# Output projection as seven products of half blocks, and norm 2 of two row tiles at a time

## The chip, the cores and the metric

The kernel runs on one core of one Trainium2 chip. The metric is device microseconds of one execution. Before the change the median of three runs is 676.44 us (676.13 to 676.68). Engines are called PE (matrix multiplies), DVE (vector), ACT (scalar), POOL (GpSimd) and SP (sync). SP and POOL issue nearly all transfers here; the transfers that add to what lies at their destination are issued by POOL.

## The reference

One decoder layer in fp32, 512 tokens, width 1024, followed by a final norm. Cut to what matters here:

```python
D_MODEL, SEQ, D_FF = 1024, 512, 2816
merged = (sigmoid(ga) * (out_a @ w_branch_swa)        # branch A
          + sigmoid(gd) * (out_d @ w_branch_diff))    # branch D
x = x + gate1 * (merged @ w_out)                      # the output projection
h2 = rmsnorm(x, norm2_g) * (1.0 + scale2) + shift2    # norm 2
u = h2 @ w_up                                         # up projection, 1024 x 5632
a, g = split(u, 2)
a = causal_depthwise_conv(a, conv_w, conv_b)
x = x + gate2 * ((gelu(a) * g) @ w_down)              # down projection
return rmsnorm(x, final_g)
```

`gate1`, `scale2`, `shift2` and `gate2` come from the conditioning vector, one value for each of the 1024 channels.

## The kernel before, in words

**Splitting.** Every fp32 operand is split in two parts (`split`, L119-120): ACT casts it into a rounded part (hi), DVE takes hi from the operand (lo). A product is then three matmuls: hi by hi, hi by lo, lo by hi. So weights go through four steps: load, ACT cast, DVE lo, PE.

**Ahead of the projection.** For each k of eight (128 channels of `merged`), a unit of gate products (`pgd`, `add_gate_d`, L953) and a unit of branch products (`pB`, `add_merge`, L963) run on PE. The merge of k (L982-984) is done on DVE and ACT: (tanh + 1) times the product, plus branch A's part `ta`, split into `mg..h` and `mg..l`.

**The output projection.** The eight rows of `w_out` (`wo`, 128x1024 each) are loaded by SP (L1025), multiplied by gate1 laid out along the rows (`g1b`, DVE, L1026) and split. `out_step(t, k)` (L1251-1260) multiplies row tile t (128 tokens) by row k of the weights into the two banks of t, called `oc`; there are eight banks, all of PSUM. Five of the eight k run over all four tiles, then the last three (`TAIL`) run tile after tile, so that tiles end one after the other: 8 x 4 x 2 x 3 = 192 matmuls of 128x512.

**Norm 2.** As a tile ends, DVE adds its banks to the residual `x1` (`add_x`, L1266); ACT squares both halves and sums the squares (`square2`, L1272); ACT takes the root (`norm_a`, L172), and a chain of small DVE operations gives the reciprocal root (`norm_b`, L174-178, L164-168). `norm_c` scales the tile into `xn` (L1286). PE turns two tiles at a time (`turn2`, L1296, banks `th`), ACT and DVE modulate and split them (`early`, L1304-1321). The last two tiles are scaled by halves on DVE and ACT (`norm_halves`).

**The up projection** already is in seven products of halves (Strassen's scheme in Winograd's form): for each of 11 column pairs J, the slots p1, m5, m6, p2, m7, p3, p4 (`mul_slot`, L1200), each 24 matmuls of 128x256. Their weights are blocks of `w_up` and sums of blocks: `s1` and `s3` are loaded by SP and added to by an accumulating transfer of POOL (`load_raw`, L1100-1102), and the sums for m6 and p3 are made in place by DVE (`sum_w`, L1124). `cast_w` (L1130, ACT) and `low_w` (L1134, DVE) split them. **The down projection** is in seven products too, with weights `chain_..` that grow by accumulating transfers (L1801).

**What sets the order.** Up to the five first k of the projection a scheduler orders the instructions. From L1333 on (`manual_schedule`) PE, DVE, ACT and POOL run in the order in which the code is written, to the end of the column pair J = 1. An engine takes its instructions in that order; one that waits holds up all behind it. SP's loads start when the buffer they write is free.

Of the kernel before, what the change touches and what calls it, by code (L numbers as in the profile page):

```python
# [8 lines left out]
F32 = mybir.dt.float32  # L9
# [5 lines left out]
P = 128  # L15
# [11 lines left out]
WB = 3  # L27
# [20 lines left out]
def kernel(  # L48
# [86 lines left out]
    hold = cpool.tile([P, 1], F32, name="hold")  # L135
# [802 lines left out]
    mg = [[bp.tile([P, 2, S], F32R, tag="gx", bufs=5, name=f"mg{i}{b}") for b in "hl"] for i in range(2)]  # L938
    mg += [[bp.tile([P, 2, S], F32R, tag="gx", bufs=5, name="mg2h"), bp.tile([P, 2, S], F32R, tag="y", name="mg2l")]]
    mg += [[bp.tile([P, 2, S], F32R, tag="fgb", name="mg3h"), gpart(5, [P, 2, S], "mg3l", F32R)]]  # L940
    mgh, mgl = ([mg[k // 2][b][:, k % 2] for k in range(KT)] for b in range(2))
    tdall = gpart(2, [P, 3, S], "tdall")
    tds, merged = {}, []

    g1b = gpart(4, [P, D], "g1b")
# [7 lines left out]
    def add_gate_d(j):  # L953
        def gate(wts):
            o = fbank(f"pgd{j}")
            yield from steps(o, wts, hT, KT)
            tds[j] = tdall[:, j % 3]
            nc.scalar.activation(tds[j], o, AF.Tanh, scale=0.5)

        units.append((lambda: load_tile(TILE_GD + j, f"wgd{j}"), gate))  # L960

    def add_merge(j):
        def load():  # L963
            if j % 2 == 0:
                r = raw_tile([P, 4, 2 * P], f"wbd{j}")
                nc.sync.dma_start(r, wbd[:, j * P : (j + 2) * P].rearrange("(i p) n -> p i n", p=P))
                if j % 4:
                    wb = bp.tile([P, 2, 4, 2 * P], F32R, tag="m5w", name=f"wbd{j}")
                else:
                    wb = gpart(3, [P, 2, 4, 2 * P], f"wbd{j}", F32R)  # L970
                wh, wl = wb[:, 0], wb[:, 1]
                casts[0], lows[0] = split(wh, wl, r)
                recent[:] = recent[1:] + lows
                pair_w["d"] = wh, wl
            return pair_w["d"]

        def branch(wts):
            o = sbank(f"pB{j}")
            rhs = [[vv[b][:, k] for k in range(4)] for b in range(2)]
            yield from steps(o, wts, rhs, 4, cl=slice(j % 2 * P, j % 2 * P + P))  # L980
            td = tds[j]
            merged.append(nc.vector.scalar_tensor_tensor(td, td, 1.0, o, ALU.add, ALU.mult))  # L982
            nc.vector.tensor_add(td, td, ta[:, j])
            split(mgh[j], mgl[j], td)

        units.append((load, branch))

    for j in range(KT):
        add_gate_d(j)
        if j:  # L990
            add_merge(j - 1)
    add_merge(KT - 1)
    while units or loaded or current or later:
        fill(1)
    root_table(tds[KT - 1][:, 0:1])
    for _ in ada:
        fill(1)
    while later:
        fill(1)
    man.close()  # L1000


    def brow(dst, src):
        nc.gpsimd.dma_start(dst, src.partition_broadcast(P))

    TAIL = 3
    xnp = [gpart(i, [P, 2, D], f"xn{i}") for i in range(2)]
    nc.vector.tensor_add(late_mod[:, 8:24], late_mod[:, 8:24], blate[:, 8:24])
    nc.vector.scalar_tensor_tensor(a2c, a2c, 1.0, n2g, ALU.add, ALU.mult)
    nc.vector.tensor_scalar_mul(a2c, a2c, -0.5)  # L1010
    x1 = big.tile([P, NT, D], F32, tag="qa", name="x1")
    for t in range(NT):
        nc.sync.dma_start(x1[:, t], xd[t * P : (t + 1) * P, :])

    def eight(name):
        return [
            [tbank(name + "0"), tbank(name + "1")],
            [fbank(name + "2"), fbank(name + "3")],
            [sbank(name + "4"), sbank(name + "5")],
            [sbank(name + "6"), vbank(name + "7")],  # L1020
        ]

    def load_rows(src, k, name, gate):
        r = raw_tile([P, D], name)
        nc.sync.dma_start(r, src[k * P : (k + 1) * P, :])  # L1025
        nc.vector.tensor_mul(r, r, gate)  # L1026
        return split_pair(r, [P, D], name)

    def tok_proj(acc, lh, ll, wts, nk, done, half_done=None):
        def step(k, t, hfs=(0, 1)):  # L1030
            wh, wl = wts[k]
            a = lh(k)[:, t * P : (t + 1) * P]
            b = ll(k)[:, t * P : (t + 1) * P]
            for hf in hfs:
                sl = slice(hf * S, (hf + 1) * S)
                nc.tensor.matmul(acc[t][hf], a, wh[:, sl], start=k == 0, stop=False)
                nc.tensor.matmul(acc[t][hf], a, wl[:, sl], start=False, stop=False)
            for hf in hfs:
                sl = slice(hf * S, (hf + 1) * S)
                nc.tensor.matmul(acc[t][hf], b, wh[:, sl], start=False, stop=k == nk - 1)  # L1040

        for k in range(nk - TAIL):
            for t in range(NT):
                step(k, t)
# [21 lines left out]
    def add_and_stat(acc, dst, x, wpool, name):  # L1066
# [12 lines left out]
        return rs  # L1079

# [800 lines left out]
```

## Time and profile before

| | |
|---|---|
| median of three runs | 676.44 us |
| the profiled execution | 676.2 us |
| its span in the trace | 674.2 us |
| mean granted PE clock | 0.997 |
| PE busy, of the span | 99% |
| DVE, ACT, POOL busy | 84%, 60%, 13% |
| first product of the output projection starts | 291.85 us |
| its last product starts | 336.17 us |
| bytes moved | 121.78 MB |

Times in the trace count from the start of the span. The profiled execution's own time is 2.0 us longer than its span, and 0.24 us under the median. A group's line names the code line, the engine, the operation, output and inputs, and the shapes. PE's busy time counts a matmul as long as it is in the pipeline, so that consecutive matmuls overlap: the distance from one start to the next is what one costs.

### The profile page before, as it was taken

The page shows a single profiled execution, that of the slowest core. Times are in us where ns is not written, and L with a number is a line of the kernel's source. Part 1 is how long each engine was busy: PE and PEld are TensorE (multiplying, and loading weights), DVE is VectorE, ACT ScalarE, POOL GpSimd, SP SyncE. Part 2 cuts the span into 40 slices and gives each one's busy share as a digit, 9 for nine tenths or more (in the row PEclk, how much of TensorE's full clock was granted, in tenths as well). Part 3 has the DMA queues.
Part 4 walks back from the last instruction along what each step waited for, and adds up shares of the span by engine and source line. Part 5 has one row for each costly group of instructions (what it writes and reads, how often), then busy time and mean ns, then how long its engine had stood idle before and what let it go on. Part 6 is the DMA issues. An engine that isn't in the chain of part 4 may idle for free.

```text
span 674.2 us, 10799 instructions
## 1 busy us (share of the span) xinstructions
PE 664.3 (99%) x4021; PEld 591.7 (88%) x4021; DVE 564.0 (84%) x1006; ACT 401.3 (60%) x705; POOL 85.0 (13%) x111
## 2 busy tenths in 40 slices
PE   8999999999999999999999999999999999999995
PEld 8888888888888888888899999999999998888884
DVE  6988987768777686644899999899889999979996
ACT  7678787465745333233696655556655666665664
POOL 2000000002212100000010211011111004441200
PEclk9999999999999999999999999999999999999998
DMA  9961231445356783367275898997887758997803
GB/s 355 418 238 62 95 95 63 137 145 180 90 168 214 229 306 117 102 181 256 77 120 155 204 203 221 243 227 187 213 212 210 203 188 217 202 206 202 158 0 125
DMA packets 72212, 121.78 MB, mean 181 GB/s; under 512 B 4256, under 2 KB 48448, under 8 KB 72160
## 3 DMA queue, kind: packets, MB, share of 16 engines
q1 hardware_dynamic: 53248, 95.04, 41.3%
q0 software_dynamic: 18624, 25.84, 22.6%
q8 instruction: 31, 0.51, 0.3%
q10 hardware_dynamic: 288, 0.21, 0.1%
q14 instruction: 21, 0.17, 0.1%
HBM read 118.97 MB, written 2.11 MB: 180 GB/s over the span
## 4 chain that ended last, share of the span: by engine, by line
PE 88%; issue 7%; DVE 2%; DMA 2%; POOL 1%; ACT 0%; POOLq 0%
PE up L1200 33%; PE dc L1815 7%; PE av L375 3%; PE pga L123 2%; PE pga L125 2%; PE pga L124 2%; PE pgd L125 2%; PE pgd L123 2%; PE oc L1260 2%; PE oc L1256 2%; PE oc L1257 2%; PE pgd L124 2%; PE aqa L372 2%; PE sd L683 2%; PE sw L585 1%
## 5 line engine op out<-in xcount | busy, mean ns | idle before, releaser
L1200 PE MATMUL up<-t,m_whi 128*128 128x256 f32 x512 | 93.1, 283 | 0.0
L1200 PEld LDWEIGHTS up<-t,m_whi 128*128 128x128 f32 x512 | 79.9, 192 | 0.0
L1200 PE MATMUL up<-t,m_wlo 128*128 128x256 f32 x256 | 72.4, 283 | 0.0
L1200 PE MATMUL up<-bh,p_whi 128*128 128x256 f32 x232 | 65.7, 283 | 0.0
L1200 PE MATMUL up<-bl,p_whi 128*128 128x256 f32 x232 | 65.7, 283 | 0.0
L1200 PE MATMUL up<-bh,p_wlo 128*128 128x256 f32 x232 | 65.7, 283 | 0.0
L1200 PEld LDWEIGHTS up<-t,m_wlo 128*128 128x128 f32 x256 | 49.2, 192 | 0.0
L1102 POOL DMA_DIRECT2D s<-in_w_up_dram x21 | 27.0, 1363 | 158.5 <-DMA s<-in_w_up_dram 95.2
L1200 PEld LDWEIGHTS up<-bh,p_whi 128*128 128x128 f32 x232 | 44.5, 192 | 0.0
L1200 PEld LDWEIGHTS up<-bl,p_whi 128*128 128x128 f32 x232 | 44.5, 192 | 0.0
L1200 PEld LDWEIGHTS up<-bh,p_wlo 128*128 128x128 f32 x232 | 44.5, 192 | 0.0
L1130 ACT CAST m_whi<-s 128x1024 fp32r<-128x1024 f32 x31 | 32.5, 1048 | 18.4 <-DVE s L1124 10.5
L1134 DVE TENSOR_TENSOR m_wlo<-s,m_whi 128x1024 fp32r<-128x1024 f32 x31 | 37.8, 1219 | 1.3 <-ACT m_whi L1130 1.3
L1200 PE MATMUL up<-t,p_whi 128*128 128x256 f32 x176 | 32.2, 283 | 0.0
L799 DVE CUSTOM_DVE_ANT_0 ra<-ra,csb 128x1024 f32<-128x1024 f32 x24 | 29.1, 1220 | 1.3 <-DMA ra<-in_w_ada_t_dram 1.3
L1200 PEld LDWEIGHTS up<-t,p_whi 128*128 128x128 f32 x176 | 27.4, 192 | 0.1
L1130 ACT CAST p_whi<-wa 128x1024 fp32r<-128x1024 f32 x18 | 18.8, 1044 | 14.0 <-PE up L1200 8.6
L709 ACT ACTIVATE sd<-sd,dmx 128x128 f32<-128x128 f32 (+3 forms) x32 | 17.7, 555 | 14.9 <-DVE dmx L694 14.7
L1134 DVE TENSOR_TENSOR p_wlo<-wa,p_whi 128x1024 fp32r<-128x1024 f32 x18 | 22.0, 1222 | 4.0 <-ACT p_whi L1130 3.3
L1200 PE MATMUL up<-t,p_wlo 128*128 128x256 f32 x88 | 24.9, 283 | 0.0
L1124 DVE TENSOR_TENSOR s<-s,wa 128x1024 f32<-128x1024 f32 x20 | 24.4, 1219 | 0.1
L1207 ACT ACTIVATE gT<-a,cols 128x512 f32<-128x512 f32 x22 | 17.5, 812 | 10.1 <-DVE a L1242 9.7
(553 smaller groups left out, 2047.9 us busy)
## 6 DMA issues: line engine op xcount, KB each, us to landing
ra<-in_w_ada_t_dram SPq DMA_DIRECT2D x24, 512.0 KB, 3.9
wa<-in_w_up_dram SPq DMA_DIRECT2D x22, 512.0 KB, 4.5
s<-in_w_up_dram SPq DMA_DIRECT2D x21, 512.0 KB, 5.5
s<-in_w_up_dram POOLq DMA_DIRECT2D x21, 512.0 KB, 7.3
adaw<-in_w_ada_t_dram SPq DMA_DIRECT2D x15, 512.0 KB, 9.8
a<-in_w_up_dram SPq DMA_DIRECT2D x11, 512.0 KB, 4.8
b<-in_w_down_dram SPq DMA_DIRECT2D x10, 512.0 KB, 4.7
w<-in_w_first_dram SPq DMA_DIRECT2D x8, 512.0 KB, 9.9
```

Of the source, the lines that this page charges most:

```text
L123: nc.tensor.matmul(o, lh, rh, start=start, stop=False)
L124: nc.tensor.matmul(o, lh, rl, start=False, stop=False)
L125: nc.tensor.matmul(o, ll, rh, start=False, stop=stop)
L375: nc.tensor.matmul(acc[i], ht[:, t : t + P], wts[k][w][:, S:], start=start, stop=stop)
L709: nc.scalar.activation(pm[m], pm[m], AF.Exp, bias=mx[:, m : m + 1], scale=-1.0, accum_out=(l0, l1)[m])
L799: nc.vector.tensor_tensor_reduce(r, r, csb, 1.0, 0.0, ALU.mult, ALU.add, late_mod[:, idx : idx + 1])
L1102: nc.gpsimd.dma_start(dst, upblock(*blk), accum_op=ALU.add)
L1124: nc.vector.tensor_add(src, src, R[J, "a11" if name == "m6" else "a12"])
L1130: nc.scalar.copy(W[J, name][0], R[J, SRC[name]])
L1134: nc.vector.tensor_sub(lo, R[J, SRC[name]], hi.bitcast(F32))
L1200: nc.tensor.matmul(o[u], w[:, k, cu], b[:, k], start=name in ("p1", "m5", "p2") and k == 0 and x == 0, stop=k == 3 and x == 2, skip_group_ ...
L1815: nc.tensor.matmul((bank2[u] if o is None else o)[:, sl], a[:, q, cu], b[:, q, sl], start=first_mm and x == 0, stop=last_mm and x == 2, sk ...
```

## The change

**Seven products.** `merged` is a 2x2 array of blocks of 512 channels by 256 tokens, `w_out` one of 512x512 blocks. The products m1, m5, m6, p2, p3, m7 and p4 (`prods`, `mul_out`) have 24 matmuls of 128x512 each, 168 in all. Each multiplies a sum of blocks of `merged` by a sum of gated blocks of `w_out`, into one of three pairs of banks: `oU` (m1, m6, m7 and p4, which accumulate on each other), `oV` (m5, p3) and `oX` (p2). Results that more than one block of the output needs are kept: `keep_sum` copies a pair of banks on ACT, and an accumulating transfer adds the copy to `x1`. `merge_x` adds or subtracts a bank in `x1` on DVE, in the place of `add_x`.

**Activations.** The merge of k writes into `M` (the buffers `outh` and `outl`), with one half of the tokens sign-changed; sums of its blocks are made on DVE, and the operands split into `a11`, `a2h`/`a2l`, `opA` and `opB`.

**Weights.** Blocks of 256x512 are loaded by SP, each gated once (`gate_o`, DVE): two of b11 into `chain_o`, two of b12 that go on to a scratch in DRAM, and two each of b22 (`p3raw`) and b21 (`p2raw`). `add_by_dma` makes the sums: POOL issues a transfer that adds one buffer, or the scratch, to another. `piece` splits a sum; the next block is added to the same buffer after that.

**Norm 2** runs on tiles 0 and 1 together, then 2 and 3: statistics two columns wide, the root by `norm_start` on ACT, the rest by `norm_end` (`rstd_end`, L163-168, in its form of several columns).

**Up projection.** For J = 0 the sums for m6 and p3 are made by accumulating transfers, in place of `sum_w`. The slot p1 of J = 1 is whole, its slot p2 stands behind m6 of J = 0. The POOL copy into `hold` is gone. Splits of the first weights (`early_w`) now stand under the branch products.

On PE the end of the projection reads as follows before (the last products of tile 2, the first of tile 3, the transposes `th0` of tiles 0 and 1; `oc4` to `oc7` are the banks of tiles 2 and 3).

```order
L1260 MATMUL oc4_2811<-wo7_h_2867,mg3l_2342 128x512
L1260 MATMUL oc5_2812<-wo7_h_2867,mg3l_2342 128x512
L1256 MATMUL oc6_2813<-wo5_h_2853,mg2h_2339 128x512
L1257 MATMUL oc6_2813<-wo5_l_2854,mg2h_2339 128x512
L1260 MATMUL oc6_2813<-wo5_h_2853,mg2l_2340 128x512
L1296 MATMUL th0_0_3128<-ident_69,xn0_2795 128x128 x4
L1296 MATMUL th0_1_3133<-ident_69,xn0_2795 128x128 x4
L1256 MATMUL oc6_2813<-wo6_h_2860,mg3h_2341 128x512
```

And now (the end of m7, whose weights are `t3p1`; the first half of p4, with weights `t4p0` and `t4p1`; the transposes):

```order
L1178 MATMUL oU1_2879<-t3p1_wlo_3082,op_hhA_2884 128x512
L1178 MATMUL oU1_2879<-t3p1_whi_3081,op_hlA_2885 128x512
L1178 MATMUL oU0_2878<-t4p0_3116,a2h0_2338 128x512 x2
L1178 MATMUL oU0_2878<-t4p0_3116,a2l0_2340 128x512
...
L1178 MATMUL oU0_2878<-t4p1_wlo_3132,a2h1_2339 128x512
L1178 MATMUL oU0_2878<-t4p1_whi_3131,a2l1_2341 128x512
L1293 MATMUL th0_0_3157<-ident_69,xn0_2840 128x128 x4
L1293 MATMUL th0_1_3162<-ident_69,xn0_2840 128x128 x4
L1178 MATMUL oU1_2879<-t4p0_3116,a2h0_2338 128x512 x2
```

The transposes stood among products into another tile's banks; now they stand between the two halves of p4, which adds to the banks that m7 has just written.

On DVE the first adds to `x1` and the norm of tile 0 read as follows before (`sso` are sums of squares, `ms` and `r0` steps of the reciprocal root, `rso` the root).

```order
L1266 TENSOR_TENSOR x1_2800<-x1_2800,oc0_2807 128x512
L1266 TENSOR_TENSOR x1_2800<-x1_2800,oc1_2808 128x512
L1342 TENSOR_TENSOR early2_2873<-wa1_0_2879,early2_2873 128x1024
L1274 TENSOR_SCALAR sso00_3051<-sso00_3051 128x1
L174 SCALAR_TENSOR_TENSOR ms_3059<-sso01_3055,sso00_3051 128x1
L178 RECIPROCAL r0_3057<-r0_3057 128x1
L164 SCALAR_TENSOR_TENSOR rt_3064<-r0_3057,ms_3059 128x1
L168 SCALAR_TENSOR_TENSOR rso0_3062<-rt_3064,r0_3057 128x1
L1286 TENSOR_SCALAR xn0_2795<-x1_2800,rso0_3062 128x1024
L1266 TENSOR_TENSOR x1_2800<-x1_2800,oc2_2809 128x512
```

And now, from the second pair of merges (out of `oV`) on:

```order
L1257 TENSOR_TENSOR x1_2873<-x1_2873,oV0_2880 128x512
L1257 TENSOR_TENSOR x1_2873<-x1_2873,oV1_2881 128x512
L1275 SCALAR_TENSOR_TENSOR ms2_0_3127<-sso01_3121,sso00_3111 128x2
L120 TENSOR_TENSOR t4p1_wlo_3132<-chain_ofgb_2343,t4p1_whi_3131 128x1024
L1283 RECIPROCAL r02_0_3129<-r02_0_3129 128x2
L165 TENSOR_TENSOR rt_3137<-r02_0_3129 128x2
L166 TENSOR_TENSOR rt_3137<-rt_3137,ms2_0_3127 128x2
L167 SCALAR_TENSOR_TENSOR rso0_3135<-rt_3137,r02_0_3129 128x2
L1257 TENSOR_TENSOR x1_2873<-x1_2873,oU0_2878 128x512
L1257 TENSOR_TENSOR x1_2873<-x1_2873,oU1_2879 128x512
L1406 TENSOR_SCALAR xn0_2840<-x1_2873,rso0_3135 128x1024
```

The reads of `oU` (tiles 2 and 3) follow the norm of tiles 0 and 1 and the lo of p4's second half.

On POOL the transfers of this stage were these (gate1's rows, the sums for J = 0 and 1, the copy):

```order
L108 DMA g1b_2344<-g1d_2422 128x1024
L1102 DMA s1_t1_2883<-in_w_up_dram 128x4x256
L1381 COPY hold_79<-ms_3168 128x1
L1102 DMA s3_0_3255<-in_w_up_dram 128x4x256
L1102 DMA s1_1_3258<-in_w_up_dram 128x4x256
L1102 DMA s3_1_3263<-in_w_up_dram 128x4x256
```

Now they are these, from m7's weights on (`b12g` is the scratch, `g1b` holds a kept sum by then):

```order
L955 DMA p3raw0_2860<-b12g0_2350 128x2x512
L955 DMA x1_2873<-g1b_2344 128x2x512
L955 DMA p3raw1_2863<-b12g1_2351 128x2x512
L1380 DMA s1_t1_2345<-in_w_up_dram 128x4x256
L992 DMA s3_0_3291<-in_w_up_dram 128x4x256
L992 DMA s1_1_3294<-in_w_up_dram 128x4x256
L992 DMA s3_1_3299<-in_w_up_dram 128x4x256
L1501 DMA s1_t1_2345<-in_w_up_dram 128x4x256
```

Ahead of the first of these stand ten more that are new: two into the scratch, six into `chain_o`, and two kept sums.

The core of the diff:

```diff
+    M = [big.tile([P, 4, S], F32, tag=g, name=f"merged_{g}") for g in ("outh", "outl")]
+    chain_o = [bp.tile([P, 2, S], F32, tag=g, name=f"chain_o{g}") for g in ("y", "fgb")]
+    def add_by_dma(dst, src):
+        nc.gpsimd.dma_start(dst, src, accum_op=ALU.add)
+    def gate_o(t, c):
+        nc.vector.tensor_mul(t, t, g1b[:, None, S * c : S * c + S].to_broadcast([P, 2, S]))
+    def gate_b12(p):
+        r = raw_tile([P, 2, S], f"b12raw{p}")
+        nc.sync.dma_start(r, wblock_o(0, 1, p))
+        gate_o(r, 1)
+        nc.gpsimd.dma_start(scratch_o(p), r)
...
+    def piece(name, p, src, home):
+        pieces[name, p] = home
+        split(home[0], home[1], src)
+    piece("m1", 0, chain_o[0], own_home("m1p0"))
+    add_by_dma(chain_o[0], scratch_o(0))
+    piece("m1", 1, chain_o[1], ring_home("m1p1"))
+    add_by_dma(chain_o[1], scratch_o(1))
+    piece("m5", 0, chain_o[0], ring_home("t1p0"))
+    add_by_dma(chain_o[0], braw["p3", 0])
...
-    def out_step(t, k, hfs=(0, 1)):
-            nc.tensor.matmul(oacc[t][hf], a, wh[:, sl], start=k == 0, stop=False)
+    def mul_out(name, us=(0, 1), ps=(0, 1)):
+                        nc.tensor.matmul(
+                            o[u], a(k, u), w[:, q], start=name in ("m1", "m5", "p2") and k == 0 and x == 0,
...
-        nc.vector.tensor_add(x1[:, t, sl], x1[:, t, sl], oacc[t][hf])
+        nc.vector.tensor_tensor(x1[:, t, sl], x1[:, t, sl], bank, op)
...
+    def keep_sum(dst, bank2, t, hf, sign):
+        for u in range(2):
+            nc.scalar.activation(dst[:, u], bank2[u], AF.Copy, scale=sign)
+        add_by_dma(x1[:, t : t + 2, hf * S : (hf + 1) * S], dst)
...
+    piece("m5", 1, chain_o[1], ring_home("t1p1"))
+    add_by_dma(chain_o[1], braw["p3", 1])
+    piece("m6", 0, chain_o[0], own_home("t2p0"))
+    keep_sum(c1, oU, 0, 0, 1.0)
+    add_by_dma(chain_o[0], braw["p2", 0])
+    mul_out("m5")
+    piece("m6", 1, chain_o[1], ring_home("t2p1"))
+    add_by_dma(chain_o[1], braw["p2", 1])
...
+    piece("p3", 0, braw["p3", 0], own_home("b22p0"))
+    add_by_dma(braw["p3", 0], scratch_o(0))
+    mul_out("p2")
+    keep_sum(c2, oU, 0, 1, -1.0)
+    piece("p3", 1, braw["p3", 1], ring_home("b22p1"))
+    add_by_dma(braw["p3", 1], scratch_o(1))
+    nc.gpsimd.dma_start(R[0, "s1"], upblock(0, 0, 0), accum_op=ALU.add)
+    mul_out("p3")
+    piece("m7", 0, braw["p3", 0], ring_home("t3p0"))
+    piece("m7", 1, braw["p3", 1], ring_home("t3p1"))
+    hi_early(2)
+    lo_early(2)
+    mul_out("m7")
+    square2(0, 0)
+    square2(1, 0)
+    piece("p4", 0, chain_o[0], own_home("t4p0"))
+    norm_first(0, 0)
+    for u in range(2):
+        merge_x(u, 1, oV[u], ALU.subtract)
+        square2(u, 1)
+    norm_start(0, 1)
+    piece("p4", 1, chain_o[1], ring_home("t4p1"))
+    rs = norm_end(0)
+    merge_x(2, 1, oU[0], ALU.subtract)
+    merge_x(3, 1, oU[1], ALU.subtract)
+    mul_out("p4", us=(0,))
     tps = {g: turn2(0, g) for g in (0, 1)}
+    mul_out("p4", us=(1,), ps=(0,))
...
+    nc.gpsimd.dma_start(R[0, "s1"], upblock(0, 0, 1), accum_op=ALU.add)
     mul_slot(0, "m6")
-    sum_w(0, "p3")
-    cast_w(0, "p3")
+    mul_slot(1, "p2")
```

More of the change, by code (lines that the diff above doesn't have):

```diff
@@ L951 @@
     after(G1_AT, lambda: to_rows(g1b, G1COL, KT, "g1"))
[L953 to L1021, printed above, removed]
@@ L1276, in norm_a @@
[L1276 to L1290 removed]
+    xns = {}
```

391 lines of the change are left out of this document (220 added, 171 removed).

## The prediction

> **What bounds the kernel now.** I read the page first, then the waits of the matmul engine (PE), then three windows, then timelines. The page's busy times and its chain of work that ended last:
>
> ```profile
> PE 664.3 (99%) x4021; PEld 591.7 (88%) x4021; DVE 564.0 (84%) x1006; ACT 401.3 (60%) x705; POOL 85.0 (13%) x111
> PE 88%; issue 7%; DVE 2%; DMA 2%; POOL 1%; ACT 0%; POOLq 0%
> ```
>
> PE is busy for 664.3 of 674.2 us, and the chain runs over it. Its waits, all of them, and the windows of the stage (columns: window, length, busy time of PE, PEld, DVE, ACT, POOL, granted clock, DMA share, GB/s):
>
> ```profile
> PE ava L241 <- POOL ones L131: 1.1, 1, 1.1
> PE av L375 <- ACT hThA L361: 0.6, 1, 0.6
> PE aka L267 <- DVE cols L271: 0.4, 1, 0.4
> ...
> 292.00:345.00 53.00, 53.00 (x274) 45.01 (x273) 33.37 (x59) 26.84 (x48) 4.10 (x4) 1.00 0.63 180
> 345.00:378.00 33.00, 33.00 (x277) 32.92 (x276) 31.28 (x44) 25.11 (x41) 2.57 (x2) 1.00 0.61 145
> ```
>
> The three waits lie far ahead of the output projection. From there on PE never waits: a matmul removed shortens the time by its own length, and a wait added lengthens it by its own, since no later idle time gives anything back. DVE and ACT have 20 and 26 us free between 292 and 345. So the question is whether the seven products keep PE fed.
>
> **What is removed.** PE's timeline, the first and the last product of the old projection, and two rows of the up projection behind it:
>
> ```profile
> 291.85 0.39 PE L1256 MATMUL oc<-wo_h,mg0h 128*128 128x512 f32 x1
> 292.08 0.39 PE L1257 MATMUL oc<-wo_l,mg0h 128*128 128x512 f32 x1
> ...
> 336.17 0.39 PE L1260 MATMUL oc<-wo_h,mg3l 128*128 128x512 f32 x1
> 336.40 1.03 PE L1296 MATMUL th<-ident,xn 128*128 128x128 f32 x8
> 337.19 0.36 PE L1200 MATMUL up<-bh,early 128*128 128x256 f32 x1
> ...
> 341.58 1.04 PE L1296 MATMUL th<-ident,xn 128*128 128x128 f32 x8
> ```
>
> Matmuls of 128x512 follow each other 0.227 us apart. 192 become 7 x 24 = 168 of the same shape: 24 x 0.227 = **-5.4 us**, all on the path. One slot of the up projection (mul_slot) is 24 matmuls of 128x256; one slot and a half, 36 of them, stand between 337.19 and 341.58: 0.122 each, 2.9 a slot.
>
> **What the other engines do in turn.** Rows that price the links, DVE and ACT:
>
> ```profile
> 297.59 1.28 ACT L182 ACT_TABLE_LOAD   x1
> ...
> 320.25 1.04 ACT L120 CAST early<-wa 128x1024 fp32r<-128x1024 f32 x1
> 321.20 1.04 ACT L1338 CAST early<-wa 128x1024 fp32r<-128x1024 f32 x1
> 324.51 0.63 ACT L1272 ACTIVATE sqo<-x 128x512 f32<-128x512 f32 x1 [2.26 <-DVE x L1266]
> 325.05 0.19 ACT L1272 ACTIVATION_READ_ACCUMULATOR sqo<-x 128x1 f32 x1
> 325.26 0.63 ACT L1272 ACTIVATE sqo<-x 128x512 f32<-128x512 f32 x1
> 326.37 0.29 ACT L172 ACTIVATE r<-sso,sso 128x1 f32<-128x1 f32 x1 [0.38 <-DVE sso L1274]
> 339.04 0.55 ACT L1306 ACTIVATE braw<-th,late_mod 128x256 f32<-128x256 f32 x1
> 339.61 0.62 ACT L1319 CAST bh<-braw 128x512 fp32r<-128x512 f32 x1
> ```
>
> ```profile
> 321.52 1.22 DVE L120 TENSOR_TENSOR early<-wa,early 128x1024 fp32r<-128x1024 f32 x1
> 322.66 1.22 DVE L1124 TENSOR_TENSOR s_t<-s_t,wa 128x1024 f32<-128x1024 f32 x1
> 323.79 1.28 DVE L1266 TENSOR_TENSOR x<-x,oc 128x512 f32<-128x512 f32 x2
> 326.69 0.16 DVE L178 RECIPROCAL r<-r 128x1 f32<-128x1 f32 x1
> 327.41 0.75 DVE L1286 TENSOR_SCALAR xn<-x,rso 128x1024 f32<-128x1024 f32 x1
> ```
>
> An ACT cast of a 128x1024 tile takes 1.05 (0.95 from start to start), a DVE operation on it 1.22 (1.14), an add of a bank into x1 0.65, a square with its sum 0.75 from start to start, a root 0.3, a small norm operation about 0.17, a modulated quarter ("act" in the code) 0.55, a cast of 128x512 ("hi") 0.62. Transfers, kind by kind (KB each, median us from issue to landing), the spread for one tile, and POOL issuing three in a row:
>
> ```profile
> s<-in_w_up_dram POOLq DMA_DIRECT2D x21, 512.0 KB, 7.3
> wo<-in_w_out_dram SPq DMA_DIRECT2D x8, 512.0 KB, 3.2
> chain_kvA<-in_w_down_dram POOLq DMA_DIRECT2D x6, 512.0 KB, 8.5
> s_t<-in_w_up_dram POOLq DMA_DIRECT2D x1, 512.0 KB, 6.0
> ...
> DMA to landing us min/median/max: 5.0/7.7/9.6
> ...
> 335.59 3.92 POOL L1102 DMA_DIRECT2D s<-in_w_up_dram  x3 [0.35 <-ACT braw L1306]
> ```
>
> The 5.0/7.7/9.6 are chain_kvA's transfers, eight, six of them accumulates. An accumulate alone on its queue takes 6.0 (s_t), one behind others 8.5; POOL issues one every 1.3. The Trainium skill (DMA: Bandwidth & Descriptors, "Anatomy of one DMA — SWDGE (gpsimd) path") fits such a transfer as 2.0 us plus its bytes over 436 GB/s, by which 512 KB would take an estimated 3.2 us. No median of the trace's accumulates is near that, so I go by the rows. By the page's price the three hand-offs below and p3's would vanish and the sum be some +5.
>
> **The hand-offs of weights.** A buffer must be split (its lo part read) before the next block may be added to it, and the sum lands 6 us or more later; then ACT casts, PE starts, and after one matmul PE needs lo, 1.22 behind the cast: a late hand-off costs its lateness and about 1.0 more.
> - m6, second half. From the end of the last branch product: four DVE operations 2.0, ACT cast 0.6, table load 1.3, two small ACT steps 0.7, cast 1.05, lo 1.22 = 6.9; landing 6.0; cast 1.05: 13.9, with the hand-overs some 14.2. PE covers it with 60 matmuls (m1, m5, half m6), 13.6. Late by 0.6, and lo: **1.6**.
> - m7, first half. From the lo of m6's second half DVE does seven operations of 128x1024 (8.0) up to the lo of p3's first half; landing 6.0, cast 1.05: 15.05. PE meanwhile: 1.2 for that lo, then 11 + 48 matmuls (m6's rest, p2, p3) = 14.6. Late 0.45, and lo: **1.45**.
> - m7, second half. Its sum is third in POOL's row, behind m7's first half and the kept sum of m5: issued 2.6 later and landing in 8.5, not 6.0: 5.1 after the first. PE spends 1.0 + 12 matmuls = 3.7. Late 1.4, and lo: **2.4**.
>
> The bounds are landings of 5.0 and 9.6 (the row): each of the three then costs about 0.6 (m7's second half 0) or 5.
>
> **p4 waits for DVE.** p4 adds to the banks oU that merge_x(2,1) and merge_x(3,1) must read first; on DVE these now stand behind norm 2 of tiles 0 and 1. From the landing of m7's last sum: ACT casts it and early_outl, squares two half tiles, casts p4's first half: 0.95 + 0.95 + 0.75 + 0.75 + 1.05 = 4.45. DVE: its lo 1.14, norm_first 0.07, two merges 1.28: 6.95. ACT squares the second merge 0.8; norm_start 0.15, root 0.3: 8.2. The cast of p4's second half follows the root, 1.05, its lo 1.14: 10.4. Four small norm operations 0.65, one merge 0.65: 11.7. PE over the same time: cast 1.05, one matmul, 1.0 for lo, 11 matmuls: 4.8. **Wait 6.8.** Nothing covers it: PE's order has p4 next. Before, the rows at 323.79 stood ahead of the norm, each tile had banks of its own and PE had the next row tile's products.
>
> **The clock.** It is the mean granted clock ahead of the last two numbers of a window's row; the last matmul, and the first ones of the kernel:
>
> ```profile
> 668.00:670.00 2.00, 0.00 (x0) 0.00 (x0) 1.75 (x7) 1.28 (x4) 0.11 (x1) 1.00 0.69 262
> 670.00:671.00 1.00, 0.00 (x0) 0.00 (x0) 0.00 (x0) 0.00 (x0) 0.48 (x1) 0.73 0.45 157
> 671.00:674.00 3.00, 0.00 (x0) 0.00 (x0) 0.00 (x0) 0.00 (x0) 0.00 (x0) 0.50 0.34 125
> ...
> 666.15 0.28 PE L1815 MATMUL dc<-p4wh,p4a 128*128 128x256 f32 x1
> ...
> 1.13 4.26 PE L241 MATMUL ava<-ones 128*128 128x128 f32 x20 [1.13 <-POOL ones L131]
> 6.69 3.99 PE L309 MATMUL av<-ones,sq 128*128 128x128 f32 x32
> ```
>
> PE ends at 666.4 and the clock halves at 670.5, 4 us on. A wait of 6.8 passes that, the shorter ones don't. What coming back costs I take from the start: 20 matmuls took 4.26, at the later pace (3.99 / 32) they would take 2.49. **+1.8**; bounds 0 (p4's wait under 4) and 2.1 (half of those 4.26).
>
> **Behind p4.** Tiles 2 and 3: after p4's last matmul ACT and DVE do in turn a merge, two squares 1.5, three modulated quarters 1.5, two hi 1.2, a lo 0.65, the root 0.3, four small steps 0.7 and xn 0.75: 7.3; PE has transposes 0.8 and two slots 5.8 meanwhile; 0.7 late, and its second row tile 0.8 after the first: **1.5** (0 to 3, as PE finds its transposes). p3 of the up projection's first column pair: its weights' sum was one DVE operation (1.22, the row at 322.66); now POOL adds a block from memory once m6's lo is done: 6.65 (between the rows of 6.0 and 7.3), cast 1.05, against m6 and p2 (moved between), 2 x 2.9, and 0.6 before they start: 1.3 late, and lo 1.0: **2.3** (0.5 to 5). m6 and m7 there come 0.3 to 0.5 late each for a cast or lo on full engines (DVE 31.28 of 33): **1.0**, from 0 to 2.
>
> At nothing I cost: gates, casts and the block copies ahead of 292 (earlier, under the branch products), the kept sums (their x1 is read 10 us and more later), the hold copy. The splits added (six pieces, four operand tiles: some 11 us on DVE, 9.5 on ACT, and 3.6 for keep_sum) fit the 20 and 26 us free; without that room they would come on top of the waits above, a few us more.
>
> **Sum.** -5.4 + 1.6 + 1.45 + 2.4 + 6.8 + 1.8 + 1.5 + 2.3 + 1.0 = +13.45. The profiled execution took 676.2 (span 674.2), 0.24 under the median: 689.65, and **689.9** against the median of 676.44.
>
> **Rivals.** A measurement of this kernel tells about 0.2%, 1.35 us, from no change.
> - *Quick sums, only p4 waits* (0.13): hand-offs at the 5.0 end, p3's too: -5.4 + 0.6 + 0.6 + 0 + 6.8 + 1.5 + 0.5 = +4.6, with the clock +6.4: 681 to 683. For it: the 5.0 row. Against: the medians. The Trainium skill's 3.2 us (DMA: Bandwidth & Descriptors, same section) would fall in here.
> - *Transfers collide* (0.15): SP loads x1 (four tiles), s3 and s1 just when the sums run. For it: the 9.6 row. Two to four landings at 9.6 add 7 to 14: 697 to 703.
> - *DVE and ACT run ahead, faster* (0.07): p4's chain takes half of 11.7, because root, squares and casts fall into gaps of m7; then p4 waits 1, the sums land in time, and some 2 us of waits remain: 676.4 - 5.4 + 2 = 673. It decides once all waits together stay under 5.4. Against: merge_x(2,1) stands behind four alternations of ACT and DVE in a written order.
> - *No change* (0.04): waits of 4 to 7 in all, or a PE stream that is not 24 matmuls shorter; 676.4.
>
> The forecast holds 0.61. **Range** 680 to 703: from quick sums with p4's wait 1 shorter (676.4 + 3.6) to the collisions' upper end; left out are faster, no change and some 0.08 beyond both ends. Faster 0.07, same 0.04, slower 0.89.
>
> **What would show it.** Right: PE with 3997 instructions; among PE's waits p4's on DVE's merge of oU, near 6.8, the largest, with a granted clock under 1 just behind it; waits of 1 to 2.5 on m6's and m7's casts and lo; the accumulates of chain_o and p3raw landing in 5 to 8.5. Wrong: no PE wait over 3 us between 295 and 380; landings near 3; or p4 starting right behind m7, for then DVE's order isn't what holds it.

## The result, and the profile after

The changed kernel takes **704.6 us** (median of four runs, 704.4 to 705.5) against 676.3 for the kernel before (676.1 to 676.7): ratio 1.0421, 95% interval 1.0403 to 1.0439. Slower was the likely side; the size, 28.3 us in place of 13.5, lies above the range. Its profiled execution has a span of 702.6 us. Busy times, granted clock and the chain that ended last, from the page of the profile after:

```profile
PE 674.0 (96%) x3997; PEld 594.3 (85%) x3997; DVE 575.6 (82%) x1028; ACT 413.5 (59%) x722; POOL 101.1 (14%) x125
PEclk9999999999999999988889999999999999999999
PE 35%; issue 9%; DVE 3%; DMA 2%; POOL 1%; ACT 1%; POOLq 0%; SPq 0%; DVEq 0%; ACTq 0%
```

PE has its 24 matmuls fewer, and yet is busy 9.7 us longer; the clock falls under full speed in four slices, 17.6 us each, from 299 to 369 us. The chain's 35% PE can't be set beside the 88% of before: it could be followed back only as far as 342.91, about half of the span. From there to p4's first product at 351.55 it runs over ACT and DVE: a cast of p4's weights, squares, the root, a split and a merge. PE's waits in this kernel (columns: total us, times, longest):

```profile
PE oU L1178 <- DVE x L1257: 5.4, 1, 5.4
PE oU L1178 <- ACT t2p_whi L120: 3.6, 1, 3.6
PE oU L1178 <- DVE t3p_wlo L120: 1.5, 2, 0.8
PE oV L1178 <- ACT op_hhA L120: 1.3, 1, 1.3
PE oU L1178 <- ACT t3p_whi L120: 1.2, 1, 1.2
PE up L1202 <- ACT p_whi L1020: 1.2, 1, 1.2
...
PE oV L1178 <- ACT t1p_whi L120: 1.0, 1, 1.0
PE oV L1178 <- DVE t1p_wlo L120: 1.0, 2, 0.8
PE up L1202 <- DVE p_wlo L1024: 0.8, 1, 0.8
```

`t1p`, `t2p`, `t3p` are the split weights of m5, m6, m7. p4's wait is the largest, as forecast, and smaller than forecast; m5, to which the prediction gave no wait, waits four times. These waits alone do not explain 28 us. What does is seen when one follows backward who had waited for whom. POOL's sums of weights, in order of time (start, time on POOL, and in brackets the idle time before it and its releaser):

```profile
283.59 1.24 POOL L955 DMA_DIRECT2D chain_ofgb<-b12g  x1 [17.07 <-DVE m1p_wlo L120]
291.74 1.24 POOL L955 DMA_DIRECT2D chain_oy<-b12g  x1 [6.91 <-DVE m1p L120]
300.60 0.88 POOL L955 DMA_DIRECT2D chain_oy<-p3raw  x1 [7.63 <-DVE t1p_wlo L120]
307.47 0.85 POOL L955 DMA_DIRECT2D chain_ofgb<-p3raw  x1 [5.99 <-DVE t1p_wlo L120]
...
326.32 1.22 POOL L955 DMA_DIRECT2D p3raw<-b12g  x1 [4.05 <-DVE b22p L120]
327.06 1.71 POOL L955 DMA_DIRECT2D x<-g1b  x1
327.87 2.14 POOL L955 DMA_DIRECT2D p3raw<-b12g  x1
```

ACT's casts, each of which waited for one of these transfers to land (or stood behind one that did):

```profile
298.00 1.04 ACT L120 CAST t1p_whi<-chain_oy 128x1024 fp32r<-128x1024 f32 x1 [3.71 <-DMA chain_oy<-b12g]
...
304.88 1.04 ACT L120 CAST t1p_whi<-chain_ofgb 128x1024 fp32r<-128x1024 f32 x1
...
316.84 1.04 ACT L120 CAST t2p_whi<-chain_ofgb 128x1024 fp32r<-128x1024 f32 x1 [7.96 <-DMA chain_ofgb<-p3raw]
...
339.54 1.04 ACT L120 CAST t3p_whi<-p3raw 128x1024 fp32r<-128x1024 f32 x1 [4.20 <-DMA p3raw<-b12g]
```

And DVE, whose split ends free the buffer for the next sum:

```profile
290.22 1.22 DVE L120 TENSOR_TENSOR m1p<-chain_oy,m1p 128x1024 fp32r<-128x1024 f32 x1
...
299.08 1.23 DVE L120 TENSOR_TENSOR t1p_wlo<-chain_oy,t1p_whi 128x1024 fp32r<-128x1024 f32 x1 [3.60 <-ACT t1p_whi L120]
...
300.82 0.68 DVE L1072 SCALAR_TENSOR_TENSOR merged_outl<-merged_outl,pB 128x512 f32<-128x512 f32 x1
...
305.95 1.23 DVE L120 TENSOR_TENSOR t1p_wlo<-chain_ofgb,t1p_whi 128x1024 fp32r<-128x1024 f32 x1 [0.25 <-ACT t1p_whi L120]
...
350.72 1.29 DVE L1257 TENSOR_TENSOR x<-x,oU 128x512 f32<-128x512 f32 x2
```

Read together, this is one chain. The sum issued at 291.74 is cast at 298.00 (6.3); splits and the last merge follow, up to the sum issued at 307.47 (9.5); its cast comes at 316.84 (9.4); then eleven microseconds, nearly all of them DVE's splits, lead to the last sum, third in POOL's row, at 327.87 (11.0), which is cast at 339.54 (11.7); then come m7's second half, the norm and the merge that lets p4 start, at 351.55 (12.0). That is 59.8 us from 291.74, 27.3 of them from the issue of a sum to its cast. PE's work in the same stretch, m1 to m7, is 144 matmuls of 0.227, 32.7 us. So between m1 and p4 PE no longer sets the time. PE's first product, p4's first, and the up projection's first show the sum of it (columns as in the timelines above):

```profile
292.73 0.62 PE L1178 MATMUL oU<-m1p,a11h 128*128 128x512 f32 x2
...
351.55 1.19 PE L1178 MATMUL oU<-t4p,a2h 128*128 128x512 f32 x2 [5.42 <-DVE x L1257]
...
360.56 0.37 PE L1202 MATMUL up<-bh,early_kvA 128*128 128x256 f32 x1
```

The up projection begins 23.4 us later than before (337.19), and the down projection 28.7 later (589.77 against 561.11). What stands behind that takes as long as it did (112.9 us to the end of the span against 113.1).

### The profile page after: what moved, and what is told of

Its sections match the earlier page's. It is cut to its first block, busy times and chain, and to the rows that moved or that the text cites. A ratio compares the mean times of both kernels' runs of the same rounds, so it can differ in the third digit from the quotient of the medians.

```text
span 702.6 us, 10831 instructions
## 1 busy us (share of the span) xinstructions
PE 674.0 (96%) x3997; PEld 594.3 (85%) x3997; DVE 575.6 (82%) x1028; ACT 413.5 (59%) x722; POOL 101.1 (14%) x125
## 4 chain that ended last, share of the span: by engine, by line
PE 35%; issue 9%; DVE 3%; DMA 2%; POOL 1%; ACT 1%; POOLq 0%; SPq 0%; DVEq 0%; ACTq 0%
PE up L1202 28%; PE dc L1868 6%; DMA s_t<-in_w_up_dram 1%; PE oU L1178 1%; DMA s<-in_w_up_dram 1%; POOL b L1854 1%; DVE p2wl L120 0%; DVE p_wlo L1024 0%; ACT sqo L1266 0%; DVE p2a L120 0%; DVE chain_kvB L1728 0%; DVE chain_outl L1730 0%; POOL s L992 0%; DVE p3wl L120 0%; DVE t4p_wlo L120 0%
## 5 line engine op out<-in xcount | busy, mean ns | idle before, releaser
L992 POOL DMA_DIRECT2D s<-in_w_up_dram x21 | 29.0, 1504 | 181.1 <-DMA s<-in_w_up_dram 76.7
L1202 PE MATMUL up<-t_kvB,m_whi 128*128 128x256 f32 x176 | 32.5, 284 | 0.2 <-DVE t_kvB L1324 0.2
L1202 PE MATMUL up<-t_outl,p_whi 128*128 128x256 f32 x176 | 32.2, 283 | 0.5 <-DVE pairs L1242 0.5
L1202 PE MATMUL up<-t_outh,m_whi 128*128 128x256 f32 x176 | 32.2, 283 | 0.0
L1202 PE MATMUL up<-t_kvA,m_whi 128*128 128x256 f32 x160 | 29.3, 283 | 0.0
L1202 PEld LDWEIGHTS up<-t_kvB,m_whi 128*128 128x128 f32 x176 | 27.5, 192 | 0.7 <-DVE t_kvB L1324 0.4
L1202 PEld LDWEIGHTS up<-t_outl,p_whi 128*128 128x128 f32 x176 | 27.4, 192 | 0.7 <-issue 0.7
L1202 PEld LDWEIGHTS up<-t_outh,m_whi 128*128 128x128 f32 x176 | 27.4, 192 | 0.0
L1202 PE MATMUL up<-t_outh,m_wlo 128*128 128x256 f32 x88 | 25.0, 284 | 0.3 <-DVE m_wlo L1024 0.3
L1202 PEld LDWEIGHTS up<-t_kvA,m_whi 128*128 128x128 f32 x160 | 24.9, 192 | 0.0
```

The lines of the kernel that those rows point to most:

```text
L992: nc.gpsimd.dma_start(dst, upblock(*blk), accum_op=ALU.add)
L1202: nc.tensor.matmul(o[u], w[:, k, cu], b[:, k], start=name in ("p1", "m5", "p2") and k == 0 and x == 0, stop=k == 3 and x == 2, skip_group_ ...
```

## The experiments

Two theories stood at the start. **Theory A**: the chain of sums, splits and casts sets the time from m1 to p4; idle time and slow clock on PE are what one sees of it. **Theory B**: each wait adds by itself, and so does the slow clock that follows. For B spoke an account from PE alone, with the lost time of the slow clock (10 us, below) in it. Unless said otherwise, the times are medians of two to four runs; the runs of one kernel lie 0.1 to 3.2 us apart, and each experiment stands against 704.6 and the kernel before, 676.4 to 676.7.

**PE kept busy in its waits.** Matmuls whose result nobody reads fill the gaps (5 behind m1, 5, 14 and 5 between the halves of m5, m6 and m7, 22 ahead of p4), so that the clock stays up.

```diff
+    def busy(n):
+        for _ in range(n):
+            nc.tensor.matmul(idle, a2h[0][:, 0, :P], a2h[0][:, 0], start=True, stop=True, skip_group_check=True)
...
-    mul_out("m6")
+    mul_out("m6", ps=(0,))
+    busy(14)
+    mul_out("m6", ps=(1,))
```

> The changed kernel with 51 products of 128x512 into a bank that nobody reads, placed on PE where it waits (5 ahead of m5's first half, 5 ahead of its second, 14 in m6, 5 in m7, 22 ahead of p4), so that PE stays busy in the waits. Changed kernel: 704.6 us; its clock is halved for 23.9 us in five stretches. Theory A (the waits are set by a chain of transfers, casts and lo parts that does not depend on PE, so a slow PE only arrives later at a wait that ends when it ends): all five stretches go, but only the halved products behind p4's wait stood on the path, 1.9 us: 702 to 703. Theory B (waits and halved clock add up): 9.9 us of slowed products go: 694 to 696. If the waits are filled too long it is slower than 704.6.

Measured 702.4 (701.5 to 703.2), ratio 1.038 (1.035 to 1.042). The clock was at half speed for 6.8 us in place of 23.9, and only 2.3 us came back: theory A. The first matmuls of m6's second half and of p4 in this kernel, from PE's timeline:

```profile
316.81 0.50 PE L1178 MATMUL oU<-t2p_whi,op_hhA 128*128 128x512 f32 x1 [1.85 <-ACT t2p_whi L120]
...
350.36 0.70 PE L1178 MATMUL oU<-t4p,a2h 128*128 128x512 f32 x2 [1.57 <-DVE x L1257]
```

With the full clock and 51 matmuls more they start only 1.1 and 1.2 us earlier than in the changed kernel (317.94 and 351.55), for they wait for the chain. Its first sum was issued 0.8 us earlier in this execution, at 290.94; from there to p4's first product it is 59.4 us, against 59.8. Most of what came back lies behind p4's wait: from p4's first product to the up projection's it is 7.3 us, against 9.0.

**p4's order.** The merges out of `oU` stand ahead of the norm on DVE, p4's second cast ahead of it on ACT, and the transposes behind p4's first 18 matmuls.

```diff
+    pieces["p4", 1] = ring_home("t4p1")
+    nc.scalar.copy(pieces["p4", 1][0], chain_o[1])
...
-    norm_start(0, 1)
-    piece("p4", 1, chain_o[1], ring_home("t4p1"))
-    rs = norm_end(0)
     merge_x(2, 1, oU[0], ALU.subtract)
     merge_x(3, 1, oU[1], ALU.subtract)
+    V.tensor_sub(pieces["p4", 1][1], chain_o[1], pieces["p4", 1][0].bitcast(F32))
+    norm_start(0, 1)
+    rs = norm_end(0)
...
+    mul_out("p4", us=(1,), ps=(0,))
     tps = {g: turn2(0, g) for g in (0, 1)}
-    mul_out("p4", us=(1,), ps=(0,))
```

> The changed kernel with the reads of oU (tiles 2 and 3) ahead of norm 2 of tiles 0 and 1 on DVE, p4's second cast ahead of the second squares on ACT, and the first transposes behind p4's first 18 products. Theory A and B: p4 starts about 4.5 us earlier (m7 ends at 346.1, two merges, then p4, instead of 351.55), so 699 to 700.5, and 698 if the halved clock behind it goes too. Rival (the wait only moves): the transposes of tiles 0 and 1 then wait for xn, which the norm gives no earlier than before, and at most 1.5 us is gained: 703 to 704.6.

Measured 699.9 (698.6 to 701.1), ratio 1.035 (1.030 to 1.039): 4.8 us less. p4's wait fell from 5.4 to 0.8, and the wait of the transposes for `xn` grew from 0.7 to 1.6. The step was a real one, but its order was not forced.

**Half of the sums on DVE.** The four sums of `p3raw` and `p2raw` into `chain_o` lie in SBUF on both sides; here DVE adds them (1.2 us each) in place of POOL's transfers.

```diff
+    def add_by_dve(dst, src):
+        nc.vector.tensor_add(dst, dst, src)
...
-    add_by_dma(chain_o[0], braw["p3", 0])
+    add_by_dve(chain_o[0], braw["p3", 0])
...
-    add_by_dma(chain_o[1], braw["p2", 1])
+    add_by_dve(chain_o[1], braw["p2", 1])
```

> The changed kernel with four of the sums of weights (chain_o plus p3raw, chain_o plus p2raw, two halves each) made by a DVE addition in place instead of an accumulating transfer. Theory A (chain): t2p's second half is ready about 8 us earlier (its sum took 9.35 us to land, a DVE addition takes 1.2), everything that hangs on it up to p4 moves by that: 695 to 697. Theory B (each wait for itself): m6's wait of 4.05 and the 3.1 us that the halved clock costs behind it go, the later waits stay: 697 to 699. Rival (collision: the later sums get no earlier, because POOL's queue and the loads set them): under 3 us gained, 702 or more.

Measured 700.7 (700.4 to 700.9), ratio 1.036 (1.033 to 1.039). Both numbers were missed, since 4.0 us came back in place of 6 to 10: m6's wait is gone, but m5 and m7 still wait for sums with the scratch, which stay transfers here, and p4's 5.4 stays.

**Loads held back.** SP's loads of `s3` and `s1` for the up projection start behind m7's second split, not beside the sums.

```diff
+    late = [gx4("s3_0"), gx4("s1_1")]
+    for t in late:
+        V.memset(t[:, 0, 0:1], 0.0)
+    with tc.issue_after(last_a[0].ins):
+        R[0, "s3"] = load_raw(late[0], [(0, 1, 0), (0, 0, 0)])
+        R[1, "s1"] = load_raw(late[1], [(1, 1, 0), (1, 1, 1)])
...
-    load_s3(0)
-    load_s1(1)
```

`last_a` is the last load that SP issued before, of a block for the column pair J = 1.

> The changed kernel with the two loads of s3 (J = 0) and s1 (J = 1) held on SP until m7's second half is split, so that 1 MB less moves beside the sums of m6's weights. Theory of collision: the sum that m6's second half waits for lands in 6.5 to 7 us instead of 9.35, and the chain is 2 to 3 us shorter: 701.5 to 702.5. Rival (POOL's queue alone sets the landing, or x1's loads do): 704 to 705.

The lines on landing that the view of one tile ends with, `chain_ofgb`, of the changed kernel, and of this one:

```profile
DMA to landing us min/median/max: 5.9/6.1/9.3
```

```profile
DMA to landing us min/median/max: 5.1/5.9/6.1
```

The sum that took 9.3 is the one issued at 307.47, and it lands in 6.1 at most when these loads are not under way; x1's loads still are. m6's wait fell from 3.6 to 1.9. The time fell by 3.0, to 701.6 (700.5 to 702.8; ratio 1.037, 1.033 to 1.042), and the chain, from its first sum (294.12 in this execution) to p4's first product, from 59.8 to 56.3. p4's wait reads 6.9 here; it reads 6.9 also with p3 of the up projection changed (below), where the projection is as it was, so the growth over 5.4 can't be put down to this edit.

**p4's order and DVE's sums together**, the two diffs above in one kernel.

> The two edits of e2 (oU read ahead of the norm) and e3 (four sums on DVE) together. Apart they gave 699.9 and 700.65 against the changed kernel's 704.6. Theory A (one chain after the other, each link is on the path): the gains of 4.7 and 4 add, 695 to 696.5. Rival (they shorten the same stretch): no better than the better one, 699 to 700.

Measured 696.9 (696.8 to 697.1), ratio 1.030 (1.028 to 1.032): 7.7 less, of 4.8 + 4.0 = 8.8, and 0.4 above the forecast: two links of one chain, which add nearly in full.

**p3 of the up projection.** Behind p4, PE waits 1.17 for p3's cast and 0.76 for its lo; the sum of its weights is issued at 375.57. Here the block is loaded once more by SP and added by DVE.

```diff
+    again = load_raw(raw_tile([P, 4, 256], "a12again"), [(0, 0, 1)])
...
-    nc.gpsimd.dma_start(R[0, "s1"], upblock(0, 0, 1), accum_op=ALU.add)
+    V.tensor_add(R[0, "s1"], R[0, "s1"], again)
```

> The changed kernel with the sum for p3 of the up projection's first column pair made by a DVE addition from a block loaded a second time by SP, in place of the accumulating transfer behind m6. Theory (as predicted: a hand-off on PE's path, its cast and lo 2.0 us late in the changed kernel's trace): 702 to 703. Rival (DVE, busy there, passes the 1.2 us on): 704 to 705.

Measured 702.4 (702.3 to 702.5), ratio 1.038 (1.036 to 1.041): 2.2 less, the price that the prediction had given (2.3).

**All of these, and a new order.** Besides, m1's two pieces exchange buffers, m5's second piece is split ahead of the operand's second half, the kept sum moves behind the sums of weights in POOL's row, and m5's weights of the up projection are split behind p4's operand.

```diff
-    piece("m1", 0, chain_o[0], own_home("m1p0"))
+    piece("m1", 0, chain_o[0], ring_home("m1p0"))
...
-    split_quarter(opA[0][:, 0], opA[1][:, 0], q21, both)
+    split_quarter(opA[0][:, 0], opA[1][:, 0], q21, (q0,))
     piece("m5", 1, chain_o[1], ring_home("t1p1"))
...
+    split_quarter(opA[0][:, 0], opA[1][:, 0], q21, (q1,))
...
     add_by_dma(braw["p3", 1], scratch_o(1))
+    add_by_dma(x1[:, 0:2, S:], c2)
```

> All that the runs so far point to, on the changed kernel: e2, e3 and e6; m1's first half split into the ring of weights and its second half into the own buffer (so that the sum for m5's first half is issued first and early); m5's second split ahead of the last operand quarter; the split of the up projection's m5 weights moved from the middle of the chain to the time when PE runs p4; the kept sum of m6 added to x1 behind the sums of m7's weights on POOL's queue. Theory A (the chain sets the time, PE's products only fit into it): most waits go, 682 to 688. If all went, 24 products less would give 676.4 - 5.4 = 671. Rival (the time is bound by what DVE has to do, whose own work grew): 690 or more.

Measured 690.5 (690.0 to 692.8, four runs), ratio 1.0206 (1.0189 to 1.0223). The slot m5 of the up projection's first column pair has other weights here and in the next kernel: they are split after a further block has been added; the amount of work is the same, the output is not the layer's. The forecast of theory A (682 to 688) was missed at the rival's edge, because a new wait appeared:

```profile
PE oV L1181 <- ACT op_hhA L120: 4.4, 1, 4.4
PE oU L1181 <- DVE merged_outl L1075: 2.3, 2, 1.2
```

With the exchanged buffers the second sum with the scratch is issued only at 296.97, in place of 283.59, and the early cast that waits for it on ACT now stands ahead of the last tanh and the operand.

**p3 ahead of p2.** The same kernel, with p3 (whose weights wait for no sum) ahead of p2, so that the last sums could start earlier.

```diff
+    mul_out("p3")
+    piece("p2", 0, braw["p2", 0], ring_home("b21p0"))
...
-    mul_out("p3")
+    mul_out("p2")
```

> e7 with p3 run ahead of p2, so that the buffers of b22 are split and added to earlier and PE has p2 between p3 and m7. Theory (m7's hand-offs are on the path): its waits of 1 to 2 us each go, and e7's time falls by 1 to 3. Rival (p3's own split then comes too late, because DVE splits one piece after the other): a wait ahead of p3 takes their place, as fast as e7 or up to 2 slower.

Measured 698.3 (698.0 to 698.6), ratio 1.032 (1.030 to 1.034): 7.8 more than with p2 first, which neither forecast had. m7's cast is now the largest wait, and ACT's timeline shows what it stands behind:

```profile
PE oU L1181 <- ACT t3p_whi L120: 5.7, 1, 5.7
```

```profile
335.75 1.04 ACT L1347 CAST early_outh<-wa 128x1024 fp32r<-128x1024 f32 x1 [11.16 <-DMA wa<-in_w_up_dram]
336.71 1.99 ACT L120 CAST t3p_whi<-p3raw 128x1024 fp32r<-128x1024 f32 x2
```

m7's sums had landed by 331.39. Ahead of their casts in ACT's order stands that of a block of `w_up`, whose load starts when p2's first block is split: at 324.00, beside m7's sums, where with p2 first it was 318.92. It lands at 335.68.

**No sums at all.** The eight transfers that sum weights of the projection are left out; splits, products and merges remain.

```diff
-    add_by_dma(chain_o[0], scratch_o(0))
...
-    add_by_dma(braw["p3", 1], scratch_o(1))
```

> The eight accumulating transfers that sum the weights of the output projection are left out, and nothing stands in their place: each product takes the piece as it was before its sum (the output is then not the projection; the number of splits, products and merges is unchanged). Theory A, the chain of sums sets the time between m1 and p4: all waits on m5, m6 and m7 go, p4 starts by about 329 in place of 351.5, and its wait shrinks to about 2 us, because the two chains of norm 2 no longer meet the late splits on DVE and ACT; 681 to 685 in all. Rival B, as the prediction had it, the sums cost only what PE waits for them and norm 2 by pairs sets p4's wait by itself: the waits on m1 to m7 go, p4's 5.4 us stays or grows: 688 to 692. If the time falls to 674 or less, the sums alone make the whole loss.

Measured 684.4 (683.8 to 685.2, four runs), ratio 1.0115 (1.010 to 1.013). This is the experiment that sizes the cause: 20.3 of the 28.3 us come and go with the sums. Its longest waits inside the projection:

```profile
PE oU L1175 <- DVE x L1254: 2.5, 1, 2.5
...
PE oV L1175 <- ACT t1p_whi L120: 1.1, 1, 1.1
```

m6's and m7's are gone, and p4's, in an order of DVE and ACT that nothing else changed, is 2.5, not 5.4. Theory B's forecast, 688 to 692 with p4's wait kept, is wrong.

**The best order with sums.** As the kernel with all of these, but m1's pieces stay in their buffers, and the weights of m5 of the up projection are split before the further block is added.

```diff
+    prep(0, "m5", (m5w[:, 0], m5w[:, 1]))
+    nc.gpsimd.dma_start(R[0, "s1"], upblock(0, 0, 0), accum_op=ALU.add)
```

> The changed kernel with every change that helped: four sums by DVE, p4's merges and second split early, p3 of the up projection summed on DVE from a second load, the kept sum behind the sums of weights in POOL's queue, m5's weights of the up projection split after p4's operand, and t1's first rows split ahead of the second operand half, with m1's pieces left in the homes they have in the changed kernel. Theory A: p4 starts about 334, waits of about 3 us on the operand of m5, 2.5 us on p4 and 1 to 2 us each on the last sums remain: 685 to 690. Rival: the order on DVE and ACT is so tight that the moved splits come late elsewhere, as in the order with exchanged homes: 690.5 or more. In no theory does it come below the kernel before, 676.3.

Measured 688.1 (687.6 to 690.8, four runs), ratio 1.0179 (1.0155 to 1.0203): 16.5 us of the loss are gone, as theory A had it. One wait of the chain remains ahead of the others. It is there without the exchange of buffers too: between m5's first split and the last merge steps (298.58 to 304.32) DVE now makes two splits and two sums.

```profile
PE oV L1181 <- ACT op_hhA L120: 6.1, 2, 4.8
PE oU L1181 <- DVE x L1260: 2.2, 1, 2.2
```

**The floor.** No sums, with p4's order and p3's sum of the up projection from the experiments above: those two diffs and the one that leaves out the sums (eleven runs).

> As the kernel without the eight sums of weights (684.4; its output is not the projection either), and with the two repairs outside the projection's products: p4's merges and second split early, and p3 of the up projection summed on DVE from a second load. It asks whether the saved matmuls, 5.4 us, come through once every transfer that sums is free. Theory A: no, the splits, merges and the norm by pairs use up what is saved: p4's wait about 1 us, about 1 us in front of the pair of transposes, about 1 us at the start: 678 to 681, not below the kernel before. Rival: the sums are the whole loss and with them and p3's gone the change is a gain: 674 or less. If the two repairs bring nothing here: 683 or more.

Measured 678.05 (677.35 to 680.58), ratio 1.0026 (1.0017 to 1.0035). Even with every sum of weights of the projection for nothing, the 24 matmuls saved do not come through. Its profiled execution was its longest (680.6), so its waits show the kind and not the size:

```profile
PE th L1290 <- DVE xn L1445: 1.6, 1, 1.6
PE oV L1175 <- ACT t1p_whi L120: 1.4, 1, 1.4
```

PE waits for `xn` of the pair of tiles, and m5's second cast stands behind the last merge. None of the kernels run beats the kernel before.

## Why the prediction missed the size

Its terms beside what PE's rows after the change show (us):

| term of the prediction | forecast | after |
|---|---|---|
| what is removed | -5.4 | -5.4 (3997 matmuls) |
| start of the projection | 0 | 0.9 (292.73 against 291.85) |
| hand-offs to m5 | 0 | 3.3 (op_hhA 1.3, t1p 1.0 + 1.0) |
| hand-off, m6's second half | 1.6 | 4.1 (3.6 + 0.5) |
| hand-off, m7's first half | 1.45 | 0.8 |
| hand-off, m7's second half | 2.4 | 2.0 (1.2 + 0.8) |
| p4 waits for DVE | 6.8 | 5.4 |
| the clock | 1.8 | 10 (matmuls at half speed) |
| behind p4 | 4.8 | 5.3 |
| sum | 13.45 | 26.4 of 28.4 |

The remaining 2.0 lie in the steps around the waits: the ten gaps of the projection are 0.16 to 0.57 longer than the waits that the profile names (297.95 to 299.62 less one step of 0.227 is 1.44, against 1.28).

- **Right**: the 24 matmuls; that PE would wait for p4 most, because DVE and ACT take turns ahead of its merge; the price of p3 and of what lies behind p4. The experiment on p4's order bears the mechanism out. The turns, priced at 11.7, took 12.0 from m7's last sum; p4's wait came out smaller than 6.8 (11.7 less 4.8 is 6.9) because PE, at half speed, was 6.6 and not 4.8 at m7's second half. m7's hand-offs came near partly by luck: the sums landed in 7.9 and 11.6 us, not 6.0 and 8.5, but PE, slowed behind m6's wait, came later as well.
- **The step that failed is "The hand-offs of weights", at m6's second half.** It counted 13.9 us "From the end of the last branch product" to the cast and let PE cover 13.6 of it. The last branch product starts at 292.51, and the cast ends at 317.88: some 25 us. Without waits and at full clock PE would have been there at 306.3 (60 matmuls from 292.73), so the cast was late by 11.5 us and not by 0.6. m5's waits, slow matmuls and m6's wait share that delay. Three links were wrong. DVE was taken to be free when that product ended; it stood at the lo of 299.08, waiting for a cast that waited for the first sum, and took up the last merge at 300.82, some 8 us late. That sum itself was issued late, at 291.74, since m1's lo reached DVE only at 290.22. And the landing took 9.4, not 6.0. A sum that lands late holds the engine that waits for it in program order, and with it the operand of the next product: the prediction priced the wait of PE, and not that of DVE and ACT.
- **The prices of m5.** "At nothing" stood m5, by silence: its second half could have been cast early (that sum was issued at 283.59), but its cast is written behind the operand's, 304.88. The best order casts it early, and its wait moves to `op_hhA`.
- **The rival "Transfers collide"** had the place and the kind right: SP's loads of x1, s3 and s1 run beside the sum issued at 307.47, as holding the last two back shows. It gave 697 to 703. It is a part of the cause: holding these two loads alone returns 3.0 us.
- **"The clock"** went wrong twice. Its rule, that only a wait of 4 us counts, does not hold (last section). And the 10 us in the table are not a cost: with the waits filled, most of them went, and 2.3 us came back. While a chain on other engines sets the time, a slow PE uses up idle time that would be there anyway: with the clock up, the chain was 59.4 us long, against 59.8.
- **What a PE account can't tell.** The table adds up almost, and would lead to theory B. That 20.3 us hang on the sums, and p4's wait halves without them, only the kernel without sums shows.

The 8.1 us that remain without sums lie mostly behind the projection: in that trace the up projection starts 2.3 us later than before (339.44), and from there to the down projection it is 229.0 us, against 223.9 before and 229.2 in the changed kernel. So the sums made nearly all of the loss ahead of the up projection, and none of the 5 us behind its start. p3 of the up projection and p4's order return 6.3 of the 8.1 together (684.4 to 678.05). Still open: where the other 1.7 go, and the 5.4 that the missing matmuls should have won.

## What to carry to other kernels

Before trading matmuls for sums of operands, add up the chain of sum, cast, split and next sum by itself, with the waits of the engines that stand in it in program order, and compare it with PE's work for the same stretch: here 60 us against 33. A product saved on PE is worth its time only as long as PE is the longer of the two. And an account of PE's waits shows where a chain is felt, not what it is made of; leaving the suspected links out shows that.

## What the runs showed of the hardware

**The clock goes by windows of 3.41 us, and 1.5 to 1.7 us of idle time in one halved it in the next.** All changes of the granted clock inside a kernel lie on a grid of 3.41 us. Windows of the changed kernel on this grid (columns: window, length, busy time of PE, PEld, DVE, ACT, POOL, granted clock, DMA share, GB/s):

```profile
297.26:300.67 3.41, 1.89 (x7) 0.94 (x5) 1.59 (x2) 2.06 (x3) 0.07 (x1) 1.00 0.01 2
300.67:304.09 3.42, 3.36 (x8) 2.48 (x8) 3.00 (x7) 1.74 (x2) 0.82 (x1) 0.50 0.69 126
304.09:307.50 3.41, 1.64 (x6) 0.84 (x5) 2.29 (x4) 3.40 (x7) 0.03 (x1) 1.00 0.97 287
307.50:310.91 3.41, 3.41 (x9) 2.67 (x9) 2.02 (x3) 1.38 (x3) 2.41 (x3) 0.50 0.94 347
...
334.81:338.22 3.41, 2.61 (x11) 1.61 (x10) 2.42 (x3) 0.53 (x1) 0.00 (x0) 1.00 1.13 200
```

PE idles 1.52 us in the first and 1.77 in the third, each in pieces under 1.3, and each time the next window is at half speed (a matmul then takes 0.43 from start to start); after the window at 300.67, in which PE hardly idles (0.06), full speed comes back. After the 0.80 idle of the last it stays up. In the traces of the kernel before, the changed one and the eleven experiments, from PE's first matmul to its last, no full-speed window with 1.50 us idle or less was followed by half speed; of nine with 1.52 to 1.58 two were, and of 32 with 1.69 or more 31 (the other had 1.83). Out of half speed the clock came back after windows with up to 0.3 us idle, and not with 0.66 or more; 0.49 and 0.60 went different ways. The Trainium skill (TensorE: Matmul & The Clock Gate, "What's actually happening") has the clock at half after one idle window of some 3.4 us. The length of the window agrees; the condition is stricter here, since PE was at work for more than half of the window at 297.26. The prediction's 4 us, read from the end of the kernel, was a window and the time up to it.

**Sums by transfer.** The eight of the changed kernel, 512 KB each, landed 5.2 to 6.2 us (four of them), 7.9, 9.3 (beside loads), 11.6 (third in a row) and 12.8 us after issue; the prediction had expected 5 to 8.5. The price that the prediction cited as the Trainium skill's, 3.2 us (DMA: Bandwidth & Descriptors, "Anatomy of one DMA — SWDGE (gpsimd) path"), no sum came near.
